# One PSUM tile for each bank of the down products, and TensorE in source order, in a two-layer encoder step

## The chip, the cores and the metric

One core of a Trainium2 chip runs the whole program. The metric is the device time of one execution in microseconds (us); lower is better. Engines are named as in the profile: PE is TensorE (PEld its weight loads), DVE is VectorE, ACT is ScalarE, POOL is GpSimd, SP is SyncE.

## The reference

An inference step of a two-layer encoder with D_MODEL = 1024 and D_FF = 4096, for 512 tokens of a new stream and 64 of a running one. Layer 0 mixes tokens by a causal pooling mixer, layer 1 by sparse attention with an indexer; after each mixer comes a squared-ReLU MLP, each with an RMSNorm ahead and a residual add behind:

```
def _mlp(h, w_up, w_down):
    u = jax.nn.relu(h @ w_up)
    return (u * u) @ w_down
...
        x = x + y.astype(x.dtype)
        x = x + _mlp(_rmsnorm(x, norm_mlp[i]), mlp_w_up[i], mlp_w_down[i]).astype(x.dtype)
```

All arrays are float32. The change concerns the two MLPs.

## The kernel before

**Data.** The residual x lies feature-major in SBUF: eight tiles x[k] of 128 features by 576 tokens, handled in two halves of 288 tokens. To keep float32 accuracy each float32 operand is split in two parts, a rounded one and a remainder, and each product is three matmuls (high by high, high by low, low by high) for each 128 x 128 block of weights and each half of the tokens. The parts of a weight are wh (a copy on ACT, L166) and wl (a subtraction on DVE, L167; in the first two up tiles of MLP 0 on POOL). xs are the two parts of the normalised input before its scale by the row statistics.

**Stages.** The kernel runs pool_mixer, mlp(0), attention and mlp(1) one after the other; `stage` opens the SBUF pools of each. PSUM has eight banks: pool ps holds three tiles of two banks, po two tiles of one bank, for the whole kernel.

**An MLP.** `mlp` (L320) works in four chunks of D_FF. A chunk has eight up tiles: `project` (L226, matmuls on L234) takes 48 matmuls into a two-bank tile `up`. `activated` reads it on DVE (v, L327: ReLU and the scale 1/rms of each token) and squares on ACT (L328); `factors` (L335) makes, of two up tiles, the seven sums that Strassen's scheme needs (L341-348). The scale of the tokens, norm.rb, is ready late: Norm.add sums the squares of x over its eight tiles into s2 (L252; on POOL for the first ones of MLP 0, on DVE otherwise), `stats` takes column sums with ten small matmuls (L284) and 1/sqrt by ACT (rt, L301) and DVE (L303-308), `spread` puts them on all partitions (diagonals on DVE, L274; matmuls rb, L264; copy on ACT, L265). No v can be computed before that, so the first up tiles stay in PSUM until then. In the source, `stats` stands behind the first up tile, `spread` behind the second.

**The down of a chunk.** Where chunk c is below `strassen` (all four in MLP 0, three in MLP 1), down(c) multiplies by Strassen's scheme: four objects `Pair` (L359), each with seven products of 12 matmuls into three banks a, b and c. The opening makes b11 on a, t2 on b, t1 on c; then DVE reads each bank (L380 or L382 for a, L383 for b, L384 for c). The closing accumulates four more: b21 on a, t3 on b, b22 on c, t4 on b, and after each of them DVE adds the bank to the residual (L396). So b takes two products in the closing, with a read between. a and b are the two banks of one ps tile `ab`, c is a po tile. The last chunk of MLP 1 is a plain product, its final norm is in `last` (L452).

**Weights.** `made` (L170) yields units in the order of use: a block of up weights is one load of 512 KB (raw, L125) and two units; a pair of down weights is two loads (pair, L183), and POOL makes sums of their quarters (L186, L187, L191, L194) for seven units a11, s2, s1, a12, a21', s2', a22. The loads are issued from ACT's queue. Units rotate through a ring of eight buffers, so wh of a unit waits until TensorE has used the unit eight before. The raws have two buffers, and one pair is in work at a time.

**Order.** The source is a program in order; a scheduler (Tile's) then orders each engine's instructions by its own simulated time and priorities, and puts in the semaphore waits. Each engine executes its own instructions in that order. Only `with tc.manual_schedule(engines=...)` keeps the source order for the engines named, as in `last` for PE. In the MLPs before the change the scheduler orders PE: it starts the next pair's opening before the pair before has closed, begins the next up tile in the tail of a down, and starts attention's first projections in the last down of MLP 0. The statistics of MLP 0 land in the third up tile, behind 35 of its 48 matmuls, those of MLP 1 in the second, behind ten.

Of the kernel before, what the change touches and what calls it, by code (L numbers as in the profile page):

```python
# [9 lines left out]
F32 = mybir.dt.float32  # L10
# [3 lines left out]
ENG = mybir.EngineType  # L14
PSUM = bass.MemoryType.PSUM

P = 128
D = 1024
KT = D // P
# [24 lines left out]
def pool_dsa_kernel(ctx: ExitStack, tc: tile.TileContext, a, o):  # L44
    nc = tc.nc
    act, dve, pool, pe = nc.scalar, nc.vector, nc.gpsimd, nc.tensor
# [4 lines left out]
    raws = ctx.enter_context(tc.tile_pool(name="raws", bufs=2))  # L51
    norms = ctx.enter_context(tc.tile_pool(name="norms", bufs=1))
    tiny = ctx.enter_context(tc.tile_pool(name="tiny", bufs=4))
    ps = ctx.enter_context(tc.tile_pool(name="ps", bufs=3, space=PSUM))
    po = ctx.enter_context(tc.tile_pool(name="po", bufs=2, space=PSUM))
    dram = ctx.enter_context(tc.tile_pool(name="dram", bufs=1, space=bass.MemoryType.DRAM))

    count = [0]
# [1 line left out]
    def uid(s):  # L60
        count[0] += 1
        return f"{s}_{count[0]}"

    phase = {}

    @contextmanager
    def stage(**pools):

        with ExitStack() as st:
            phase.clear()  # L70
            for name, bufs in pools.items():
                phase[name] = st.enter_context(tc.tile_pool(name=uid(name), bufs=bufs, reuse_waits="tile"))
            yield

    def slot(tag, s, dt=F32R):
# [13 lines left out]
        return tiny.tile([P, n], F32, tag=s, name=uid(s))  # L89

    def psum(s="ps"):
        return ps.tile([P, 2, 512], F32, tag="ps", name=uid(s))

    def psum1(s="po"):
        return po.tile([P, 512], F32, tag="po", name=uid(s))

    def f32(t):
        return t.bitcast(F32)
# [1 line left out]
    def halves(t):  # L100
        return t.rearrange("p (h t) -> p h t", h=2)
# [108 lines left out]
    def next_block(sub=dve):  # L210
        return [next_unit(5 - i, sub) for i in range(2)]

    def at(w, k):

        return [t[:, (k % 4) * P:(k % 4 + 1) * P] for t in w[k // 4]]
# [10 lines left out]
    def project(pt, w, xs, between=iter(()), cols=((0, HT), (HT, HT))):  # L226

        n = len(xs)
        for k in range(n):
            next(between, None)  # L230
            wh, wl = at(w, k)
            for i, (wt, part) in enumerate(((wh, 0), (wh, 1), (wl, 0))):
                for h, (c, m) in enumerate(cols):
                    pe.matmul(  # L234
                        pt[:, h, :m], wt, xs[k][:, part, c:c + m],
                        start=(k == 0 and i == 0), stop=(k == n - 1 and i == 2),
                    )

    class Norm:
# [14 lines left out]
        def stats(self):  # L254
            pt = psum1("st")
            token_sums(pt, self.s2)
            self.r = rms(pt)

        def spread(self):
            diag = diagonals(self.r)  # L260
            self.rb = tmp("rb" + self.s, "rb", 1)
            for h in range(2):
                pb = psum1("rb")
                pe.matmul(pb[:, :HT], ones, diag[:, h * HT:(h + 1) * HT], start=True, stop=True)  # L264
                act.copy(self.rb[:, h * HT:(h + 1) * HT], pb[:, :HT])  # L265
            return self.rb
# [44 lines left out]
    def split_x(gi, norm, tags, add=dve):  # L311
        xs = []
        for k in range(KT):
            t = pair_slot(tags[k], "xs")
            split(t, x[k], gv[:, gi, k:k + 1])
            norm.add(k, add if k < 6 else dve)
            xs.append(t)
        return xs

    def mlp(layer, gi, strassen, add=dve, end=None):  # L320
        norm = Norm(f"m{layer}")
        xs = split_x(gi, norm, ["xs"] * KT, add)
# [7 lines left out]
        def plain(pt, u):  # L330
            v = halves(tmp("v"))
            activated(pt, v)
            split(u.rearrange("p a (h t) -> p a h t", h=2), v)
# [25 lines left out]
        class Pair:  # L359


            def __init__(self, c, q, us):
                self.c, self.q, self.us = c, q, us
                ab = psum("ab")
                self.a, self.b, self.c_ = ab[:, 0], ab[:, 1], psum1("c")
                self.lo, self.hi = ([x[2 * q + i][:, c0:c0 + HT] for i in range(2)] for c0 in (HT, 0))

            def opening(self, parts=((0, 1, 2, 3),)):
# [29 lines left out]
        def down(c, us):  # L398
            for q in range(KT // 2):
                p = Pair(c, q, us)  # L400
                for _ in p.opening(((0, 1, 2, 3),) if q else ((0, 1, 2), (3,))):
                    pass
                p.closing()
# [3 lines left out]
        def finished(c, i, pt, us):  # L407
            nonlocal v
            f = UP_ORDER[i]
            if c < strassen:  # L410
                if i % 2 == 0:
                    v = phase["acts"].tile([P, 4, HT], F32, tag="v", bufs=1, name=uid("v"))
                activated(pt, v[:, 2 * (i % 2):2 * (i % 2) + 2])
                if i % 2:
                    us[i // 2] = factors(v)
            else:
                if i % 3 == 0:
                    v = phase["u"].tile([P, 7 * 2 * HT], F32R, tag="u", bufs=4, name=uid("u"))
                us[f] = v[:, (i % 3) * SLOT:(i % 3 + 1) * SLOT].rearrange("p (h t) -> p h t", h=2)
                plain(pt, us[f])  # L420

        us = [[None] * KT for _ in range(4)]
        todo = []
        steps = [s for c in range(4) for s in [(c, i) for i in range(c > 0, 8)] + ([(c + 1, 0)] if c < 3 else []) + [(c, None)]]
        for n, (c, i) in enumerate(steps):
            if i is not None:
                w = next_block(sub=add if n < 2 else dve)
                pt = psum("up")
                project(pt, w, xs)
                todo.append((c, i, pt, us[c]))  # L430
                if n == 0:
                    norm.stats()
                    continue
                if n == 1:
                    norm.spread()
                for t in todo:
                    finished(*t)
                todo.clear()
                continue
            if c < strassen:  # L440
                down(c, us[c])
                continue
            for m in range(KT if end is None or c < 3 else KT - LAST):
                w = next_block()
                pt = psum("dn")
                project(pt, w, us[c])
                dve.tensor_tensor(halves(x[m]), halves(x[m]), pt[:, :, :HT], ALU.add)
# [675 lines left out]
            dve.tensor_tensor(x[m][:, 2 * P:], x[m][:, 2 * P:], pt[:, 0, :T - 2 * P], ALU.add)  # L1123

    x = Residual()
    with stage(slots=1, xs=1, tmps=6):
        pool_mixer()
    with stage(u=1, xs=1, acts=1, tmps=3, pairs=1, more=2):
        mlp(0, 1, 4, pool)
    with stage(slots=1, xs=1, cst2=1, tmps=6):  # L1130
        attention()
    with stage(xs=1, u=1, acts=1, tmps=3, pairs=1, more=2):
        mlp(1, 3, 3, end=last)


# [94 lines left out]
```

## Time and profile before

| | us |
|---|---|
| median of 3 runs (lowest to highest) | 1165.96 (1164.63 to 1166.82) |
| profiled execution | 1169.65 |
| its span, first to last instruction | 1167.8 |
| mean granted clock of TensorE | 0.980 |
| busy: PE / DVE / ACT / POOL | 1110.5 / 817.0 / 528.9 / 349.9 |

The span is 1.85 us shorter than the execution's own time. Rows of a timeline give start, duration, engine, line, operation, output and inputs; "x3" groups three instructions; a bracket gives the idle time of the engine before it and what ended it. In the view of one line, "its engine sat idle before it" lists total us and times by releaser. In tables of stretches come the busy times of each engine, the granted clock (1.00 is full speed), the DMA share and GB/s. L-numbers are lines of the kernel before; tile names stand without their numbers.

### The profile page before, as it was taken

The page shows a single profiled execution, that of the slowest core. Times are in us where ns is not written, and L with a number is a line of the kernel's source. Part 1 is how long each engine was busy: PE and PEld are TensorE (multiplying, and loading weights), DVE is VectorE, ACT ScalarE, POOL GpSimd, SP SyncE. Part 2 cuts the span into 40 slices and gives each one's busy share as a digit, 9 for nine tenths or more (in the row PEclk, how much of TensorE's full clock was granted, in tenths as well). Part 3 has the DMA queues.
Part 4 walks back from the last instruction along what each step waited for, and adds up shares of the span by engine and source line. Part 5 has one row for each costly group of instructions (what it writes and reads, how often), then busy time and mean ns, then how long its engine had stood idle before and what let it go on. Part 6 is the DMA issues. An engine that isn't in the chain of part 4 may idle for free.

```text
span 1167.8 us, 20621 instructions
## 1 busy us (share of the span) xinstructions
PE 1110.5 (95%) x8244; PEld 1090.6 (93%) x8244; DVE 817.0 (70%) x1478; ACT 528.9 (45%) x968; POOL 349.9 (30%) x274
## 2 busy tenths in 40 slices
PE   7999999999999999798989999999999999989995
PEld 6999999999999999797979999999999989989995
DVE  7776666767667786759999853876766767775434
ACT  5644344335334444253368665654344335333331
POOL 7711410330240351117775341101410330350002
PEclk8999999999999999798989999999999999999998
DMA  5421241232232134366652432431241132114212
GB/s 172 114 75 52 73 145 55 75 125 73 73 108 91 38 113 161 101 197 158 170 154 74 121 104 81 157 109 55 73 145 55 57 125 90 55 55 122 77 37 82
DMA packets 51152, 116.68 MB, mean 100 GB/s; under 512 B 9345, under 2 KB 22960, under 8 KB 51056
## 3 DMA queue, kind: packets, MB, share of 16 engines
q10 hardware_dynamic: 23184, 84.45, 23.1%
q1 hardware_dynamic: 27872, 30.90, 9.2%
q8 instruction: 65, 1.06, 0.4%
q14 instruction: 31, 0.25, 0.1%
HBM read 99.73 MB, written 13.25 MB: 97 GB/s over the span
## 4 chain that ended last, share of the span: by engine, by line
PE 60%; DVE 15%; issue 12%; POOL 5%; DMA 4%; ACT 3%; SPq 0%; DVEq 0%; ACTq 0%; POOLq 0%
PE up L234 30%; PE ab L356 8%; DVE wl L167 5%; PE dn L234 4%; PE pj L234 4%; PE c L356 3%; DVE work L896 2%; PE o L971 2%; DMA raw<-in_w_up 2%; PE wa L234 1%; DMA pair<-in_w_down 1%; DVE m L895 1%; POOL sum L194 1%; PE v L1088 1%; PE pb L720 1%
## 5 line engine op out<-in xcount | busy, mean ns | idle before, releaser
L234 PE MATMUL up<-xs,wh 128*128 128x288 f32 x2048 | 355.9, 295 | 1.5 <-DVE v L327 1.3
L234 PEld LDWEIGHTS up<-xs,wh 128*128 128x128 f32 x2048 | 299.8, 188 | 2.5 <-DVE v L327 1.7
L356 PE MATMUL ab<-u,wh 128*128 128x288 f32 x1120 | 227.2, 297 | 11.4 <-DVE x L396 5.8
L166 ACT CAST wh<-raw 128x512 fp32r<-128x512 f32 (+1 forms) x210 | 126.0, 619 | 206.2 <-DMA raw<-in_w_up 61.9
L234 PE MATMUL up<-xs,wl 128*128 128x288 f32 x1024 | 219.4, 295 | 0.0
L167 DVE TENSOR_TENSOR wl<-raw,wh 128x512 fp32r<-128x512 f32 (+1 forms) x186 | 144.3, 784 | 70.7 <-ACT wh L166 68.9
L356 PEld LDWEIGHTS ab<-u,wh 128*128 128x128 f32 x1120 | 179.4, 189 | 15.3 <-DVE x L396 8.6
L356 PE MATMUL ab<-u,wl 128*128 128x288 f32 x560 | 165.5, 298 | 2.0 <-DVE wl L167 1.9
L234 PEld LDWEIGHTS up<-xs,wl 128*128 128x128 f32 x1024 | 164.2, 188 | 0.0
L167 DVE TENSOR_TENSOR wl<-pair,wh 128x512 fp32r<-128x512 f32 x112 | 101.4, 917 | 30.5 <-ACT wh L166 30.0
L194 POOL TENSOR_TENSOR sum<-sum,pair 128x512 f32<-128x512 f32 x28 | 41.2, 1472 | 265.4 <-DVE wl L167 265.4
L186 POOL TENSOR_TENSOR sum<-pair 128x512 f32<-128x512 f32 x28 | 38.0, 1357 | 266.7 <-DMA pair<-in_w_down 266.7
L166 ACT CAST wh<-sum 128x512 fp32r<-128x512 f32 x84 | 51.0, 621 | 145.8 <-POOL sum L187 47.7
L356 PEld LDWEIGHTS ab<-u,wl 128*128 128x128 f32 x560 | 105.4, 189 | 3.9 <-DVE wl L167 3.5
L166 ACT CAST wh<-pair 128x512 fp32r<-128x512 f32 x112 | 68.2, 620 | 86.4 <-PE up L234 40.7
L356 PE MATMUL c<-u,wh 128*128 128x288 f32 x448 | 92.5, 295 | 0.4 <-ACT wh L166 0.4
L167 DVE TENSOR_TENSOR wl<-sum,wh 128x512 fp32r<-128x512 f32 x84 | 71.2, 858 | 26.2 <-ACT wh L166 25.4
L327 DVE SCALAR_TENSOR_TENSOR v<-up,rbm 128x576 f32<-128x576 f32 x64 | 48.2, 755 | 58.6 <-PE up L234 57.2
L234 PE MATMUL pj<-xs,wh 128*128 128x288 f32 x448 | 83.5, 304 | 4.1 <-DVE t L783 4.1
L234 PEld LDWEIGHTS pj<-xs,wh 128*128 128x128 f32 x448 | 70.1, 197 | 5.8 <-DVE t L783 4.9
L356 PEld LDWEIGHTS c<-u,wh 128*128 128x128 f32 x448 | 72.4, 189 | 0.7 <-ACT wh L166 0.7
L356 PE MATMUL c<-u,wl 128*128 128x288 f32 x224 | 66.0, 296 | 0.0
(224 smaller groups left out, 1974.6 us busy)
## 6 DMA issues: line engine op xcount, KB each, us to landing
raw<-in_w_up ACTq DMA_DIRECT2D x64, 512.0 KB, 3.6
pair<-in_w_down ACTq DMA_DIRECT2D x56, 512.0 KB, 3.6
raw<-in_w_o ACTq DMA_DIRECT2D x16, 512.0 KB, 4.1
raw<-in_w_in ACTq DMA_DIRECT2D x15, 512.0 KB, 4.0
q<-st SPq DMA_DIRECT2D x32, 144.0 KB, 2.6
q<-q SPq DMA_DIRECT2D x16, 256.0 KB, 3.0
raw<-in_w_down ACTq DMA_DIRECT2D x8, 512.0 KB, 3.5
x<-in_x SPq DMA_DIRECT2D x8, 288.0 KB, 6.3
```

Of the source, the lines that this page charges most:

```text
L166: act.copy(h, src)
L167: how["sub"].tensor_tensor(l, src, f32(h), ALU.subtract)
L186: pool.tensor_tensor(s1, a21, a22, ALU.add)
L194: pool.tensor_tensor(s2, s2, a12, ALU.add)
L234: pe.matmul(pt[:, h, :m], wt, xs[k][:, part, c:c + m], start=(k == 0 and i == 0), stop=(k == n - 1 and i == 2),)
L327: dve.scalar_tensor_tensor(v, pt[:, :, :HT], 0.0, halves(norm.rb), ALU.max, ALU.mult)
L356: pe.matmul(bank[:, :HT], wt, ut, start=first and j == 0 and i == 0, stop=last and j == 3 and i == 2, skip_group_check=True)
L720: pe.matmul(pt[:, c0:c0 + rhs.shape[1]], lhs, rhs, start=n == 0, stop=n == len(steps) - 1)
L895: dve.max(m8[:np_], wk[:np_])
L896: dve.match_replace(wk[:np_], m8[:np_], wk[:np_], TAKEN)
L971: pe.matmul(oc[:, 2 * s + hh], pT[:, c:c + P], V[:, kt, vs], start=kt == 0, stop=kt == i)
L1088: pe.matmul(pt[:n, :264], xs[k][:, part, i * P:i * P + n], wt[:, sl], start=(k == 0 and j == 0), stop=(k == KT - 1 and j == 2))
```

## The change

The pools ps and po are opened for each stage. pool_mixer and attention get ps = 3 and po = 2, as before; both MLPs get ps = 2 (two tiles of two banks) and po = 4 (four tiles of one bank): eight banks in each case. A Pair's a, b and c become three tiles of one bank. Both calls of mlp stand in manual_schedule for PE, so TensorE executes an MLP in the order of the source: a pair's seven products (the first pair's opening in two parts) before the next pair's, a down before the next up tile, and attention behind the last down. `norm.stats()` moves from behind the first up tile to the middle of the second, behind 30 of its 48 matmuls. No instruction is added or removed on any engine's work; on POOL and SP the order is nearly unchanged, on DVE and ACT it changes locally.

```diff
@@ pools and stages @@
-    ps = ctx.enter_context(tc.tile_pool(name="ps", bufs=3, space=PSUM))
-    po = ctx.enter_context(tc.tile_pool(name="po", bufs=2, space=PSUM))
...
             for name, bufs in pools.items():
-                phase[name] = st.enter_context(tc.tile_pool(name=uid(name), bufs=bufs, reuse_waits="tile"))
+                space = {"space": PSUM} if name in ("ps", "po") else {}
+                phase[name] = st.enter_context(tc.tile_pool(name=uid(name), bufs=bufs, reuse_waits="tile", **space))
...
-        return ps.tile([P, 2, 512], F32, tag="ps", name=uid(s))
+        return phase["ps"].tile([P, 2, 512], F32, tag="ps", name=uid(s))
...
-        return po.tile([P, 512], F32, tag="po", name=uid(s))
+        return phase["po"].tile([P, 512], F32, tag="po", name=uid(s))
@@ class Pair @@
-                ab = psum("ab")
-                self.a, self.b, self.c_ = ab[:, 0], ab[:, 1], psum1("c")
+                self.a, self.b, self.c_ = (psum1(t) for t in "abc")
@@ mlp @@
+        def sums():
+
+            for k in range(KT):
+                if k == KT // 2 + 1:
+                    norm.stats()
+                yield
+
...
-                project(pt, w, xs)
+                project(pt, w, xs, sums() if n == 1 else iter(()))
                 todo.append((c, i, pt, us[c]))
                 if n == 0:
-                    norm.stats()
                     continue
@@ calls @@
-    with stage(slots=1, xs=1, tmps=6):
+    with stage(slots=1, xs=1, tmps=6, ps=3, po=2):
         pool_mixer()
-    with stage(u=1, xs=1, acts=1, tmps=3, pairs=1, more=2):
-        mlp(0, 1, 4, pool)
-    with stage(slots=1, xs=1, cst2=1, tmps=6):
+    with stage(u=1, xs=1, acts=1, tmps=3, pairs=1, more=2, ps=2, po=4):
+        with tc.manual_schedule(engines={ENG.PE}):
+            mlp(0, 1, 4, pool)
+    with stage(slots=1, xs=1, cst2=1, tmps=6, ps=3, po=2):
         attention()
-    with stage(xs=1, u=1, acts=1, tmps=3, pairs=1, more=2):
-        mlp(1, 3, 3, end=last)
+    with stage(xs=1, u=1, acts=1, tmps=3, pairs=1, more=2, ps=2, po=4):
+        with tc.manual_schedule(engines={ENG.PE}):
+            mlp(1, 3, 3, end=last)
```

## The prediction

> **What bounds the kernel now.** I read the page first: the busy time of the engines.
>
> ```profile
> PE 1110.5 (95%) x8244; PEld 1090.6 (93%) x8244; DVE 817.0 (70%) x1478; ACT 528.9 (45%) x968; POOL 349.9 (30%) x274
> ```
>
> TensorE works for 95% of the span. The change keeps every matmul, so the time can move only through TensorE's idle time. What Strassen's down products wait for is in the view of line L356.
>
> ```profile
>   DVE x L396: 5.8, 11
>   ACT wh L166: 3.3, 3
>   DVE u L347: 2.1, 1
>   DVE wl L167: 1.9, 5
>   DVE x L383: 0.7, 1
> ```
>
> That is 13.8 us (the second number is how often) in seven downs. 6.5 of it (L396 and L383) are waits for VectorE to read a bank, 5.2 waits for weights, 2.1 a wait for factors. The end of a matmul in the trace is modelled, some 0.16 us after the next one's start, so each of the 20 waits besides L347's is worth 0.16 more: 8.4 us for banks, 6.5 for weights, 14.9 together. This is the most that the downs can give. L347's wait (the last factors before the down of chunk 3) depends neither on banks nor on the order, and stays.
>
> The unit of all that follows is the matmul step. A product is 12 of them:
>
> ```profile
> 225.32 0.42 PE L356 MATMUL c<-u,wh 128*128 128x288 f32 x2
> ...
> 226.90 0.42 PE L356 MATMUL ab<-u,wh 128*128 128x288 f32 x2
> ```
>
> 1.58 us, 0.132 a matmul, and 6.35 for an up tile of 48.
>
> **Part 1: the statistics of MLP 0.** Before, they are in the third up tile, after 35 of its 48 matmuls.
>
> ```profile
> 65.84 1.16 PE L284 MATMUL st<-ones,s 128*128 128x2 f32 x10
> ...
> 69.17 1.24 PE L264 MATMUL rb<-diag,ones 128*128 128x288 f32 x4 [0.25 <-DVE diag L274]
> 71.69 0.53 PE L234 MATMUL up<-xs,wh 128*128 128x288 f32 x2 [1.29 <-DVE v L327]
> ```
>
> Counted back from 65.84, the third tile began at 61.2, the second at 54.85. The change puts the statistics after 30 matmuls of the second: TensorE comes to them at 58.8. Their input s2 ends on a chain over POOL and VectorE:
>
> ```profile
> 59.89 1.88 POOL L252 TENSOR_TENSOR s<-s,sq 128x576 f32<-128x576 f32 x1
> ```
>
> ```profile
> 61.80 0.76 DVE L252 TENSOR_TENSOR s<-s,sq 128x576 f32<-128x576 f32 x1 [1.32 <-POOL s L252]
> 62.48 0.68 DVE L167 TENSOR_TENSOR wl<-raw,wh 128x512 fp32r<-128x512 f32 x1
> 63.08 0.75 DVE L252 TENSOR_TENSOR s<-s,sq 128x576 f32<-128x576 f32 x1
> ```
>
> The change keeps POOL's order here; on VectorE the wl (0.60 from start to start) no longer stands between the two adds. So s2 is there at about 63.3 rather than 63.83, and TensorE waits about 4.5 us, in order, with 18 ready matmuls of the second tile and the whole third tile behind the wait. From the statistics on the chain stays: they began at 65.84, and the next up tile 5.85 later, when a v had been written out of its PSUM buffer. It is now the third tile, not the fourth, that waits for this, because the MLPs have two buffers of two banks where there were three. With the statistics at 63.5 it starts at 69.4. Two tiles are then done; before, three were at 71.69. At 69.4 + 6.35 = 75.75 TensorE is as far as it was at 71.69: **4.1 us lost**.
>
> The clock can add to it. L347's wait of 2.1 us, and the stretches behind it (length, busy time of PE, PEld, DVE, ACT, POOL, then the granted clock):
>
> ```profile
> 401.65 0.61 PE L356 MATMUL ab<-u,wh 128*128 128x288 f32 x1 [2.06 <-DVE u L347]
> ```
>
> ```profile
> 402.00:403.00 1.00, 1.00 (x5) 1.00 (x5) 1.00 (x1) 0.62 (x1) 0.00 (x0) 0.50 0.00 0
> 403.00:404.00 1.00, 1.00 (x6) 1.00 (x6) 1.00 (x3) 0.62 (x1) 0.12 (x1) 0.50 0.03 8
> 404.00:405.00 1.00, 1.00 (x6) 1.00 (x6) 0.98 (x3) 0.79 (x2) 1.00 (x1) 0.50 0.00 0
> ```
>
> Three us at half the clock, 1.5 us of work. The new gap of 4.5 us is longer than the one before these rows, so I expect the same; as a part of the slow stretch falls into the time in which TensorE waits for rb anyway, I take 1.2, between 0 and 1.5.
>
> **Part 2: the statistics of MLP 1.**
>
> ```profile
> 757.46 0.75 DVE L252 TENSOR_TENSOR s<-s,sq 128x576 f32<-128x576 f32 x1
> ...
> 767.48 1.42 DVE L327 SCALAR_TENSOR_TENSOR v<-up,rbm 128x576 f32<-128x576 f32 x2 [0.46 <-ACT rbm L265]
> ```
>
> ```profile
> 760.53 0.33 ACTq L125 DMA_DIRECT2D raw<-in_w_up  x1
> 762.16 1.14 ACT L166 CAST wh<-raw 128x512 fp32r<-128x512 f32 x2 [2.47 <-DMA raw<-in_w_up]
> 763.21 0.40 ACT L301 ACTIVATE rt<-st,eps 128x4 f32<-128x4 f32 x2
> ```
>
> ```profile
> 758.68 1.15 PE L284 MATMUL st<-ones,s 128*128 128x2 f32 x10
> ...
> 766.64 0.90 PE L234 MATMUL up<-xs,wh 128*128 128x288 f32 x4
> ```
>
> s2 is there at 758.2; ten matmuls of the second tile stand before the statistics at 758.68, so 30 put them at 761.3 without a wait on TensorE. But ScalarE has a chain of weight loads ahead of rt. In the changed order one more wh stands there, the one whose raw is issued at 760.53 and lands some 3.6 later (row below), 764.1: rt goes from 763.2 to about 765.2, and with it diag, rb and the first v, which ended at 767.48 + 0.71 = 768.2, to about 770.1. Before, the third buffer let the third up tile start without that v, at 767.0 (within the row at 766.64); now it waits for it: **3.1 us lost**, between 1.2 (rt not delayed) and 4. Half of a slow stretch on top, 0.7, between 0 and 1.5.
>
> **Part 3: the downs.** Groups and loads that their price needs (busy, mean ns of one):
>
> ```profile
> L167 DVE TENSOR_TENSOR wl<-pair,wh 128x512 fp32r<-128x512 f32 x112 | 101.4, 917 | 30.5 <-ACT wh L166 30.0
> L194 POOL TENSOR_TENSOR sum<-sum,pair 128x512 f32<-128x512 f32 x28 | 41.2, 1472 | 265.4 <-DVE wl L167 265.4
> L186 POOL TENSOR_TENSOR sum<-pair 128x512 f32<-128x512 f32 x28 | 38.0, 1357 | 266.7 <-DMA pair<-in_w_down 266.7
> ...
> raw<-in_w_up ACTq DMA_DIRECT2D x64, 512.0 KB, 3.6
> pair<-in_w_down ACTq DMA_DIRECT2D x56, 512.0 KB, 3.6
> ```
>
> In source order a pair's last four products are b21 on bank a, t3 on b, b22 on c, t4 on b again. t4 may not start before VectorE has added t3's bank to the residual, and only b22 lies between: from t3's end VectorE has 1.58 us. The read itself is 0.45, but VectorE takes its instructions in order, and remainders of weights (L167) and the read of bank a stand before it. Such a pile did this before:
>
> ```profile
> 227.00 1.71 DVE L167 TENSOR_TENSOR wl<-sum,wh 128x512 fp32r<-128x512 f32 x2 [1.03 <-ACT wh L166]
> 228.64 1.78 DVE L167 TENSOR_TENSOR wl<-pair,wh 128x512 fp32r<-128x512 f32 x1
> 230.34 0.44 DVE L396 TENSOR_TENSOR x<-x,c 128x288 f32<-128x288 f32 x1
> 230.70 0.44 DVE L396 TENSOR_TENSOR x<-x,ab 128x288 f32<-128x288 f32 x1
> ```
>
> The product on c that ended by 227.0, and the one on ab after it, were read at 230.34 and 230.70, two to three us late. TensorE lost nothing there, because the order before had the next pair's opening (up to three products, 4.75 us) to do meanwhile. The changed order has none of it between t3 and t4: that cover is what it gives up. Per pair, from the start of its b11: second weight load issued after 0.4, landed after 4.0, two POOL sums of 1.3 (the mean of 1.36 has the slow ones of the start in it), wh 0.6 (1.14 for two, above), then in VectorE's new order wl 0.92, a's read 0.45, two wl of 0.85 (from the pile's 1.71), t3's read 0.45: 10.7. t4 is due after six products, 9.5, so it waits 1.2 us. The same walk with each pair's own order on VectorE gives 0.35 for pair 0, 1.2 (MLP 0) to 2.1 for pair 1, 0.95 to 2.2 for pair 2, and nothing for pair 3, where no sums stand in between. For the seven downs: 2.5 three times and 4.2 in MLP 0, 3.8, 3.8 and 4.65 in MLP 1: 24.0 us, where 14.9 go. **9.1 us lost.** An error of 0.5 us at each of the 21 waits moves this by 10.5 either way, and nothing excludes a gain up to the whole 14.9.
>
> The separate tiles of a, b and c let a bank go when its own read ends; that is within the 8.4 us. That attention's first projections (57 of their matmuls lay in the last down) now follow it takes none of their work away, and attention's entry waits for VectorE either way: I count nothing.
>
> **The sum.** 4.1 + 1.2 + 3.1 + 0.7 + 9.1 = 18.2. The profiled execution took 1169.65 (its span 1167.8 and 1.85 around it), so it would be 1187.85; it was 3.7 above the median of the runs, 1165.96, to which I add the same 18.2: **1184 us**.
>
> **Rivals.**
> - *The banks pay* (faster). If t3's read always ends within 1.58 us, because the sums come early enough that only reads stand before it, TensorE loses no time at t4; and products in the order in which weights are made release the ring in order, so the 6.5 us of weights go too. For it: the waits for L396 are the largest item, and VectorE is idle for 30% of the span. Against it: the pile at 227. Starts +7.2 (without the clock) to +9.1, downs −10 to −15: 1158 to 1165, taken as 1161. It decides at a wait of 0.28 us at each of the 21: at 5.8 us of new waits the downs' gain of 9.1 equals the starts' loss.
> - *The downs come out even*: new waits of 0.7 us at each of the 21. Only the starts count: 1166 + 9 = 1175.
> - *The clock follows the waits.* Five of the 21 new waits come out at 2 us or more (pair 1 in MLP 1, pair 2 in the last chunks), as long as L347's 2.1. If each of them is followed by three us at half the clock, as that one was, 5 x 1.5 = 7.5 us more: 18.2 + 7.5 = 25.7, 1192. For it: the rows at 402. Against it: one such wait in the downs before is all there is to go by, and my five are walked to 0.5 us. [...]
> - *The starts cost nothing*, if s2 were there at 59 rather than 63.3, and the downs are even: no change. POOL's add from 59.89 and the two after it speak against it.
>
> **Chances.** Forecast 0.42, its own range 1179 to 1190; even downs 0.20; clock 0.16; banks pay 0.17; starts free 0.05. A measurement of this kernel tells about 0.2%, 2.3 us, from no change. Faster 0.17, same 0.05, slower 0.78. The range reaches from the upper half of the faster case to the clock's case and a few us over it, for waits longer than walked: 1162 to 1198.
>
> **What would show it.** In the changed profile: L284 waits 4 to 5 us for DVE L252 at 59, and the third up tile starts at about 69.4 after a v (part 1); in MLP 1 rt stands at 765 and the third up tile at 770, after a v (part 2); L356 waits for x some 18 to 22 times, 0.3 to 2.2 us each, on b, and hardly for wh or wl (part 3). I am wrong if t3's reads end before b22 does, or if the waits for weights grow instead, because the sums' remainders come late in VectorE's new order.

## The result, and the profile after

The changed kernel takes 1206.64 us in the median of four runs (1202.82 to 1210.6), against 1166.39 for the kernel before (1164.63 to 1171.1): a ratio of 1.0339, 95% interval 1.0294 to 1.0384. It is about 40 us slower; 18 were forecast. The direction was right, the size was not. The profiled execution of the changed kernel took 1210.6 us, with a span of 1208.8, 41.0 more than before.

The page of the changed kernel, its head and the row of slices for the clock (tenths of full speed in 40 slices):

```profile
span 1208.8 us, 20641 instructions
...
PE 1121.2 (93%) x8244; PEld 1101.9 (91%) x8244; DVE 824.5 (68%) x1478; ACT 532.6 (44%) x968; POOL 355.6 (29%) x274
...
PEclk8989999999999998899889999999999999999998
```

The same row of the kernel before:

```profile
PEclk8999999999999999798989999999999999999998
```

PE executes the same 8244 matmuls and is busy 10.7 us longer, so some of them ran slower; there are more 8s in the clock's row, and the mean granted clock is 0.969 (0.980 before). The rest of the 41 us is idle time. What TensorE waits for (total, times, longest):

```profile
PE b L356 <- DVE x L395: 34.4, 23, 6.1
...
PE up L234 <- DVE x L1128: 3.6, 1, 3.6
PE up L234 <- DVE v L327: 3.3, 2, 1.9
PE a L356 <- DVE u L347: 3.3, 1, 3.3
PE st L284 <- DVE s L252: 3.1, 1, 3.1
```

(L395 is L396 of the kernel before, L1128 its L1123.) The forecast wait at t4 is there, on b, 23 times; no product waits for wh or wl any more. Only it is 34.4 us and not 24.0. The stages, taken from the matmuls in the timelines, show where the 41 us are; the last two columns belong to experiments below.

| stretch, us | before | changed | changed, sums on DVE | before, sums on DVE |
|---|---|---|---|---|
| pool mixer's last matmul to first down | 61.3 | 68.4 | 64.2 | 60.4 |
| first down to attention's statistics | 358.1 | 378.1 | 356.6 | 348.8 |
| these to attention's last matmul | 283.0 | 281.5 | 280.2 | 283.1 |
| attention's last matmul to MLP 1's first down | 60.3 | 66.5 | 62.6 | 59.1 |
| first down to the plain product | 290.0 | 298.9 | 289.7 | 279.5 |
| plain product to the last matmul | 58.2 | 58.5 | 58.6 | 58.6 |

The two starts lose 7.1 and 6.2 us, the downs 20.0 and 8.9. The start of MLP 0, on PE:

```profile
49.68 0.76 PE L234 MATMUL up<-xs,wh 128*128 128x288 f32 x4 [1.13 <-DVE x L733]
63.40 2.18 PE L284 MATMUL st<-ones,s 128*128 128x2 f32 x10 [3.14 <-DVE s L252]
72.41 0.77 PE L234 MATMUL up<-xs,wh 128*128 128x288 f32 x4 [1.37 <-DVE v L327]
```

The statistics stand at 63.40, where 63.5 was forecast. But the ten matmuls take 2.18 us where they took 1.16, and the third up tile comes at 72.41, not at 69.4. Stretches of the granted clock (third number from the right) say why, here and in four of the downs:

```profile
64.00:65.00 1.00, 1.00 (x6) 1.00 (x6) 0.00 (x0) 0.00 (x0) 0.00 (x0) 0.50 0.00 0
66.00:67.00 1.00, 1.00 (x6) 1.00 (x5) 0.82 (x6) 0.02 (x1) 0.00 (x0) 0.50 0.00 0
68.00:69.00 1.00, 1.00 (x6) 1.00 (x5) 0.00 (x0) 0.00 (x0) 0.00 (x0) 0.50 0.00 0
343.00:344.00 1.00, 1.00 (x6) 1.00 (x5) 0.94 (x2) 0.00 (x0) 0.00 (x0) 0.50 0.81 328
462.00:463.00 1.00, 1.00 (x6) 1.00 (x6) 1.00 (x2) 0.17 (x1) 0.00 (x0) 0.50 0.00 0
968.00:969.00 1.00, 1.00 (x6) 1.00 (x5) 0.22 (x1) 0.00 (x0) 0.00 (x0) 0.50 0.60 242
1071.00:1072.00 1.00, 1.00 (x6) 1.00 (x6) 0.42 (x2) 0.00 (x0) 0.00 (x0) 0.50 0.59 217
```

Six matmuls in a us, at half the clock, where a busy us of the up tiles at 1.00 has nine or ten. Busy time times the missing clock, summed over stretches of 1 us, is 15.1 us in the two MLPs (3.2 and 1.5 at the starts, 10.5 in the downs) against 1.6 before, all of it in one down.

One pair of the second chunk shows what t4 waits for. VectorE:

```profile
235.35 1.41 DVE L167 TENSOR_TENSOR wl<-pair,wh 128x512 fp32r<-128x512 f32 x1
236.90 1.56 DVE L167 TENSOR_TENSOR wl<-sum,wh 128x512 fp32r<-128x512 f32 x1
238.39 0.44 DVE L395 TENSOR_TENSOR x<-x,a 128x288 f32<-128x288 f32 x1
238.76 1.62 DVE L167 TENSOR_TENSOR wl<-sum,wh 128x512 fp32r<-128x512 f32 x1
240.30 0.68 DVE L167 TENSOR_TENSOR wl<-pair,wh 128x512 fp32r<-128x512 f32 x1
240.90 0.44 DVE L395 TENSOR_TENSOR x<-x,b 128x288 f32<-128x288 f32 x1
```

POOL and PE at the same time:

```profile
234.92 1.29 POOL L187 TENSOR_TENSOR sum<-sum,pair 128x512 f32<-128x512 f32 x1
236.18 1.75 POOL L191 TENSOR_TENSOR pair<-pair,pair 128x512 f32<-128x512 f32 x1
238.55 1.28 POOL L194 TENSOR_TENSOR sum<-sum,pair 128x512 f32<-128x512 f32 x1 [0.62 <-DVE wl L167]
```

```profile
239.26 0.29 PE L356 MATMUL c<-u,wl 128*128 128x288 f32 x1
241.49 0.50 PE L356 MATMUL b<-u,wh 128*128 128x288 f32 x2 [1.93 <-DVE x L395]
```

b22 is done at 239.55, t3's read ends at 241.34, t4 starts at 241.49. Ahead of the read stand four remainders. The one at 240.30, with POOL idle, takes 0.68. The three that overlap an addition of POOL take 1.41, 1.56 and 1.62, and each of them ends about 0.55 us after that addition: 236.76 after 236.21, 238.46 after 237.93, 240.38 after 239.83. They look like instructions that stand still until POOL is done. The read of a bank takes 0.44 us beside POOL and without it. The experiments ask whether this is the cause.

The longest wait of the 23, 6.08 us up to 461.05, has another beginning. The second load of its pair was issued at 444.81, and POOL's first sum could start only at 452.19, 7.4 us later (the median from issue to landing is 3.6); VectorE then sat idle for weights, and the remainders came after that.

```profile
452.19 1.29 POOL L186 TENSOR_TENSOR sum<-pair 128x512 f32<-128x512 f32 x1 [3.78 <-DMA pair<-in_w_down]
```

```profile
454.17 0.69 DVE L167 TENSOR_TENSOR wl<-sum,wh 128x512 fp32r<-128x512 f32 x1 [3.47 <-ACT wh L166]
```

Why this load took so long was not tried.

### The profile page after: what moved, and what is told of

Same layout as the page of the kernel before. It is cut to its first block, busy times and chain, and to the rows that moved or that the text cites. A ratio compares the mean times of both kernels' runs of the same rounds, so it can differ in the third digit from the quotient of the medians.

```text
span 1208.8 us, 20641 instructions
## 1 busy us (share of the span) xinstructions
PE 1121.2 (93%) x8244; PEld 1101.9 (91%) x8244; DVE 824.5 (68%) x1478; ACT 532.6 (44%) x968; POOL 355.6 (29%) x274
## 4 chain that ended last, share of the span: by engine, by line
PE 62%; issue 15%; DVE 12%; POOL 6%; ACT 3%; DMA 1%; ACTq 0%; SPq 0%; DVEq 0%; POOLq 0%
PE up L234 30%; PE b L356 5%; PE pj L234 5%; DVE wl L167 4%; PE dn L234 4%; PE a L356 3%; PE o L976 2%; PE wa L234 2%; PE c L356 2%; ACT wh L166 2%; POOL sum L187 1%; POOL sum L186 1%; DVE work L901 1%; POOL sum L194 1%; PE v L1093 1%
## 5 line engine op out<-in xcount | busy, mean ns | idle before, releaser
L167 DVE TENSOR_TENSOR wl<-raw,wh 128x512 fp32r<-128x512 f32 (+1 forms) x186 | 147.8, 798 | 79.5 <-ACT wh L166 74.2
L356 PE MATMUL b<-u,wh 128*128 128x288 f32 x672 | 142.9, 305 | 35.2 <-DVE x L395 34.4
L356 PEld LDWEIGHTS b<-u,wh 128*128 128x128 f32 x672 | 110.5, 194 | 40.9 <-DVE x L395 22.7
L186 POOL TENSOR_TENSOR sum<-pair 128x512 f32<-128x512 f32 x28 | 38.9, 1389 | 263.1 <-DMA pair<-in_w_down 237.4
L356 PE MATMUL b<-u,wl 128*128 128x288 f32 x336 | 101.4, 302 | 0.0
L356 PE MATMUL a<-u,wh 128*128 128x288 f32 x448 | 94.8, 304 | 3.3 <-DVE u L347 3.3
L356 PE MATMUL c<-u,wh 128*128 128x288 f32 x448 | 91.1, 295 | 0.0
L356 PEld LDWEIGHTS a<-u,wh 128*128 128x128 f32 x448 | 75.4, 197 | 3.5 <-DVE u L347 3.5
L356 PEld LDWEIGHTS c<-u,wh 128*128 128x128 f32 x448 | 72.0, 189 | 0.0
```

What stands on the lines that cost most here:

```text
L167: how["sub"].tensor_tensor(l, src, f32(h), ALU.subtract)
L186: pool.tensor_tensor(s1, a21, a22, ALU.add)
L356: pe.matmul(bank[:, :HT], wt, ut, start=first and j == 0 and i == 0, stop=last and j == 3 and i == 2, skip_group_check=True)
```

## The experiments

**Theories.** A: TensorE's source order takes away the cover between t3 and t4, and that is the loss. B (rival): the PSUM layout costs (two two-bank buffers, pools opened for each stage). C (rival to A, formed from the rows above): the loss comes from the weights' sums, by POOL's work beside VectorE or by lateness; the source order only uncovers it. Times are medians in the order of the runs; a ratio is to the kernel before, on the same chip.

**1 to 3. The parts alone.** 1, the layout without the order:

```diff
-                project(pt, w, xs, sums() if n == 1 else iter(()))
+                project(pt, w, xs)
...
                 if n == 0:
+                    norm.stats()
                     continue
...
-        with tc.manual_schedule(engines={ENG.PE}):
-            mlp(0, 1, 4, pool)
+        mlp(0, 1, 4, pool)
...
```

> The changed kernel with the scheduler ordering TensorE again and the statistics back in their old place: only the PSUM layout is left of the change. If the source order is what costs (theory), the waits for x L395 fall from 34.4 us to under 8 and the time is 1160 to 1172, the starts paying up to 4 us for the missing third two-bank buffer. If the layout costs (rival: two two-bank buffers, pools opened for each stage), it stays above 1185.

2, the order and the moved statistics without the layout:

```diff
...
-                project(pt, w, xs)
+                project(pt, w, xs, sums() if n == 1 else iter(()))
...
-        mlp(0, 1, 4, pool)
+        with tc.manual_schedule(engines={ENG.PE}):
+            mlp(0, 1, 4, pool)
...
```

> The kernel before with TensorE in source order in both MLPs and the statistics amid the second up tile, but with its own PSUM layout for the whole kernel. Theory: the waits at t4 are there as in the changed kernel (30 us or more for x) and the time is 1190 to 1205; less than the changed kernel only by its new waits at the entries of the MLPs (1.1 and 3.6 us). Rival (layout): under 1175.

3, only the pools opened for each stage, at their old sizes:

```diff
...
-    with stage(u=1, xs=1, acts=1, tmps=3, pairs=1, more=2):
+    with stage(u=1, xs=1, acts=1, tmps=3, pairs=1, more=2, ps=3, po=2):
...
```

> The kernel before with its PSUM pools opened for each stage, at the old sizes. If a pool that opens waits for the last reader of the pools before it, the first up tile of MLP 1 stands about 3.6 us later and that of MLP 0 about 1.1: 1167 to 1171. If the two entry waits come from the source order alone, no change, 1166.

Measured: 1187.43 us for the layout alone (1.0165, 1.0138 to 1.0191), 1250.91 for the order alone (1.0699, 1.0678 to 1.0721), 1172.21 for the pools alone (1.0040, 1.0025 to 1.0055). The first comes out where theory B has it, the second far beyond what theory A has, the third a us above its range. The order alone costs 84 us, twice the whole change. Its waits:

```profile
PE ab L356 <- DVE x L396: 48.8, 29, 4.0
PE ab L356 <- DVE x L383: 9.5, 8, 3.3
PE st L284 <- DVE s L252: 6.3, 2, 4.4
```

Where a and b are one tile, a read of one bank held up the product on the other (one t3, on b, starts at 247.12, released by the read of a that began at 246.53), and in source order nothing covers it; against this kernel the changed one is 44 us faster. So the two parts of the change are not additive. The layout alone loses 6.5 and 5.5 us in the starts, and 12.9 from MLP 0's first down to attention's statistics, where TensorE still waits for x L395 (9.0 us on b, 8 times, in both MLPs) and on c (2.6); in MLP 1's downs it gains 2.6. The pools for each stage cost 4.9: the first up tile of MLP 1 waits 3.5 us for the last read of attention's last tile, and that of MLP 0 for 1.1.

**4, 7, 12. The starts.** 4, the statistics behind all of the second up tile:

```diff
-                project(pt, w, xs, sums() if n == 1 else iter(()))
+                project(pt, w, xs)
...
                 if n == 1:
+                    norm.stats()
                     norm.spread()
```

> The changed kernel with the statistics behind all 48 matmuls of the second up tile. Theory: in MLP 0 the wait for s2 falls from 3.1 to about 0.8 us and the slow clock behind it goes, 2 to 4 us gained there; in MLP 1, where the statistics did not wait, the third up tile starts about 2 us later: 1203 to 1207 in all. Rival (the slow clock there does not hang on the wait): the clock is 0.5 from 63 on again and the time 1207 to 1211.

7, matmuls that nobody needs, in the wait for s2:

```diff
+                    if layer == 0:
+                        fill = psum1("fill")
+                        for j in range(24):
+                            pe.matmul(fill[:, :HT], xs[0][:, 0, :P], xs[0][:, 0, :HT], start=j == 0, stop=j == 23)
+                        act.copy(small(1, "fill"), fill[:, :1])
                     norm.stats()
```

> The changed kernel with 24 idle matmuls (128x288, into a one-bank tile of their own, 3.2 us) ahead of the statistics of MLP 0, where TensorE waits 3.1 us for s2 and the clock is then halved for six us. If the halved clock hangs on that wait, it stays at 1.00 there, the first down starts 2 to 3 us earlier than 68.4 us after the pool mixer's last matmul, and the time is 1203 to 1205. If it does not, the first down starts as before and the time is 1206 to 1208.

12, the order of the pools:

```diff
-    with stage(u=1, xs=1, acts=1, tmps=3, pairs=1, more=2, ps=2, po=4):
+    with stage(u=1, xs=1, acts=1, tmps=3, pairs=1, more=2, po=4, ps=2):
...
```

> The changed kernel with po opened ahead of ps in both MLPs, so that the first up tile lies on other banks than the last tiles of the stage before. If its wait at the entries (1.1 us in MLP 0, 3.6 us in MLP 1, with a slow clock behind it) is for the one tile that held those banks, it goes or shrinks: 1201 to 1205. If a new pool waits for everything before it, no change: 1206 to 1208.

Measured: 1209.31 (1.0348, 1.0326 to 1.0369), 1202.39 (1.0295, 1.0277 to 1.0313) and 1208.63 (1.0351, 1.0313 to 1.0388). The changed kernel's own interval overlaps all three. Late statistics no longer wait for s2, but then rb waits for diag and the clock is halved from 65 to 75 all the same; MLP 1's start grows from 66.5 to 72.6. With the filling matmuls the clock stays at 1.00 until the first v is waited for (1.89 us), and is halved then; the stretches of that kernel:

```profile
62.00:65.00 3.00, 3.00 (x24) 2.73 (x23) 1.14 (x6) 0.56 (x3) 0.00 (x0) 1.00 0.09 34
65.00:68.00 3.00, 2.51 (x16) 1.94 (x14) 1.85 (x5) 1.02 (x2) 0.00 (x0) 1.00 0.00 0
70.00:72.00 2.00, 2.00 (x10) 2.00 (x9) 1.79 (x5) 1.65 (x3) 0.00 (x0) 0.50 0.30 123
```

So the halved clock at 63 did follow from the idle time, as that expectation has it, but the first down comes only 0.7 us earlier (67.7 for 68.4): the slow stretch moved to the next wait. With po first the waits for L733 and L1128 are gone, and the starts are 68.7 and 66.0 us, much the same. In MLP 0 TensorE then waits 4.5 us for s2 instead. In MLP 1 rt now stands behind a wh that waits for its load:

```profile
794.58 0.62 ACT L166 CAST wh<-raw 128x512 fp32r<-128x512 f32 x1 [1.45 <-DMA raw<-in_w_up]
795.11 0.40 ACT L301 ACTIVATE rt<-st,eps 128x4 f32<-128x4 f32 x2
```

That is 3.2 us behind the start of the statistics (791.95), 1.2 in the changed kernel, and the clock falls behind the wait for v (0.57 from 800 to 804). What sets the starts is the chain to the first v, which the third up tile needs when there are only two buffers: in MLP 0 from s2 on, in MLP 1 by way of rt. To take away a wait ahead of it gains 0.7 us at most in these three runs.

**5, 6, 9, 11. The cover, and VectorE's order.** 5, the next pair's b11 between b22 and t4:

```diff
+            def first(self):
+                self.started = True
+                product(self.a, next_unit(), self.us, "b11", (0, 1, 2, 3), True, True)
...
-                    product(bank, next_unit(), self.us, factor, js, False, True)
+                    w = next_unit()
+                    if factor == "t4" and following:
+                        following.first()
+                    product(bank, w, self.us, factor, js, False, True)
```

> The changed kernel with the next pair's b11 (12 matmuls into the fourth one-bank tile, free then) put between b22 and t4, so that VectorE has 3.2 us and not 1.6 for t3's read. Theory (t4 lacks cover): of the 34.4 us of waits for x L395 only what is longer than 1.6 stays, some 10 us, and the slow clock behind the short ones goes: 1175 to 1185. Rival (VectorE and the weights are late as such): the waits move to the opening or to wh and wl, and the time stays above 1195.

6, t3 first in the closing:

```diff
+            yield split_unit(a21)
             yield split_unit(a12)
-            yield split_unit(a21)
...
-                for bank, factor, out, b2 in ((self.a, "b21", self.lo[0], 0), (self.b, "t3", self.hi[1], 0),
+                for bank, factor, out, b2 in ((self.b, "t3", self.hi[1], 0), (self.a, "b21", self.lo[0], 0),
```

> The changed kernel with t3 ahead of b21 in the closing (and the unit a21' made ahead of a12), so that two products lie between t3 and t4, but only one between t2 and t3 on the same bank. Theory: the waits at t4 go as with the cover, but t3 now waits for POOL's sum a21' and for the read of t2: 1180 to 1195. Rival: no gain, 1200 or more.

9, VectorE in source order in the downs of the changed kernel (11: of the kernel before, with VectorE alone):

```diff
+                with tc.manual_schedule(engines={ENG.PE, ENG.DVE}):
                     for _ in p.opening(((0, 1, 2, 3),) if q else ((0, 1, 2), (3,))):
                         pass
                     p.closing()
```

> The changed kernel with VectorE, too, in source order inside the downs: t3's read then stands behind one remainder after b21's read, not behind two or three. TensorE's order is the changed kernel's. If VectorE's order makes t3's read late, the waits for x fall to 10 to 15 us, some come back as waits for wl, and the time is 1180 to 1195. If the missing cover alone decides, it stays at 1200 to 1210.

> The kernel before with VectorE alone in source order inside the downs, TensorE left to the scheduler: reads of banks stand ahead of more of the remainders. If VectorE's order costs the kernel before its 8 us of bank waits too, 1158 to 1164; if the remainders then come late for TensorE instead, 1166 to 1180.

Measured: 1197.36 (1.0247, 1.0222 to 1.0271), 1191.66 (1.0198, 1.0174 to 1.0222), 1204.34 (1.0322, 1.0269 to 1.0374) and 1192.83 (1.0212, 1.0196 to 1.0227). The waits of 5:

```profile
PE b L356 <- DVE x L404: 26.8, 17, 5.2
```

(L404 is the same addition.) Twice the cover takes 7.6 of the 34.4 us away, where theory A expected 24. t3 first, with two products between t3 and t4, comes out in theory A's range: it leaves 11.0 for the closing's reads and makes 11.5 for the opening's. VectorE in source order has 23.2 for x and 5.6 for wh, and no clear gain. In the kernel before, the scheduler's order of VectorE was the better one by 24 us, more than either range of 11 had. So cover is worth something, and 6 is the best of the kernels in source order that keep the sums on POOL; but theory A in its plain form, that one product more between t3 and t4 mends it, fell here: VectorE is later than that.

**8, 10, 15. The sums taken away.** These three leave out the use of POOL's four sums of each pair: the units are made from the plain quarters, so the results are not those of the step, and only the times count. 8 and 15 have no additions (changed kernel and kernel before), 10 is the changed kernel with the additions made into tiles that nothing reads. The edit of 8 and 15:

```diff
...
-            pool.tensor_tensor(s1, a21, a22, ALU.add)
-            pool.tensor_tensor(s2, s1, a11, ALU.add)
             yield split_unit(a11)
-            yield split_unit(s2)
-            yield split_unit(s1)
-            pool.tensor_tensor(a21, a21, a11, ALU.add)
+            yield split_unit(a21)
+            yield split_unit(a21)
             yield split_unit(a12)
             yield split_unit(a21)
-            pool.tensor_tensor(s2, s2, a12, ALU.add)
-            yield split_unit(s2)
+            yield split_unit(a12)
```

> The changed kernel without POOL's sums of weights: the four additions of a pair are left out and their units are made from the plain quarters, so VectorE and ScalarE do as many splits, but nothing waits for POOL and nothing of POOL runs beside VectorE. If the waits at t4 come from the remainders that VectorE must do ahead of t3's read, late by POOL's sums and slowed beside them (the pile's wl of 1.4 to 1.8 us where I reckoned 0.85), they fall below 10 us and the time to 1170 to 1180. If the strict order of TensorE is enough by itself, more than 20 us of waits stay and the time is above 1190.

> As the run without POOL's sums (units from the plain quarters), but POOL still makes its four additions a pair into tiles that nothing reads: nothing waits for them, they only run beside VectorE. If it is the work beside VectorE that makes the pile (wl of 1.4 to 1.8 us), waits come back and the time is 1165 to 1185; if it is that the sums come late, it stays at 1153 to 1158.

> The kernel before without POOL's sums of weights (left out; units from the plain quarters), beside the changed kernel without them, 1153. If the source order costs nothing by itself once the pile is gone, this gives 1140 to 1150, that is better than 1153 by the starts alone (some 5 to 10 us); if the source order is still worth something against it, over 1155.

Measured: 1153.36 (0.9864, 0.9849 to 0.9879), 1219.83 (1.0438, 1.0419 to 1.0457) and 1140.30 (0.9750, 0.9730 to 0.9770). 8 gains more than expected, 10 loses more. What the downs wait for in 8 (the view of the products' line, with its other numbers):

```profile
  DVE x L378: 2.7, 2
  DVE x L390: 1.2, 4
  DVE u L343: 1.0, 1
```

and what TensorE waits for in 10:

```profile
PE b L356 <- DVE x L395: 30.3, 24, 3.3
PE c L356 <- DVE x L383: 15.0, 13, 1.7
```

Both have TensorE in source order, the same splits and loads, and no product that needs a sum. In 8 the waits for x are 3.9 us, in 10 they are 45.3. What differs is that POOL works beside VectorE. VectorE's order does not: by their names, 1473 of its 1478 instructions stand in the same order in both. The remainders show it; the group of 8, then that of 10:

```profile
L167 DVE TENSOR_TENSOR wl<-pair,wh 128x512 fp32r<-128x512 f32 x196 | 136.9, 707 | 64.3 <-ACT wh L166 63.8
```

```profile
L167 DVE TENSOR_TENSOR wl<-pair,wh 128x512 fp32r<-128x512 f32 x196 | 190.6, 981 | 72.0 <-ACT wh L166 72.0
```

707 ns each against 981. So it is POOL's work beside VectorE, not that the sums come late. Between 15 and 8 lie 13 us: without the pile the change still costs 2.2 and 3.1 us in the starts, 5.9 from MLP 0's first down to attention, and 1.3 or less in each other stretch. The change by itself is nearly free in MLP 1's downs (280.9 for 279.9 us).

**13, 14. The sums on VectorE.** All work is kept; 13 is the kernel before, 14 the changed one.

```diff
-            pool.tensor_tensor(s1, a21, a22, ALU.add)
-            pool.tensor_tensor(s2, s1, a11, ALU.add)
+            dve.tensor_tensor(s1, a21, a22, ALU.add)
+            dve.tensor_tensor(s2, s1, a11, ALU.add)
...
-            pool.tensor_tensor(a21, a21, a11, ALU.add)
+            dve.tensor_tensor(a21, a21, a11, ALU.add)
...
-            pool.tensor_tensor(s2, s2, a12, ALU.add)
+            dve.tensor_tensor(s2, s2, a12, ALU.add)
```

> The kernel before with the four additions of each pair of weights on VectorE and not on POOL; all work is kept. 112 additions of about 0.7 us are 78 us more for VectorE, while its 196 remainders of the downs lose what they pay beside POOL (0.89 in the mean against 0.69 alone: 39 us). If POOL's work beside VectorE is what delays reads and weights, 1155 to 1165; if VectorE becomes the bound in the downs, 1170 to 1190.

> The changed kernel with the same additions on VectorE; all work is kept. If the waits at t4 hang on POOL's work beside VectorE, they fall below 15 us and the time to 1170 to 1185, though VectorE has 78 us more to do; if they hang on the amount of VectorE's work ahead of t3's read, they stay above 30 us and the time at 1200 to 1230.

Measured: 1146.94 for 13 (0.9811, 0.9796 to 0.9827), better than expected, and 1170.93 for 14 (1.0026, 1.0009 to 1.0044). 13 beats both kernels by 1.9% and more. Its groups on VectorE:

```profile
L167 DVE TENSOR_TENSOR wl<-pair,wh 128x512 fp32r<-128x512 f32 x112 | 78.1, 704 | 23.8 <-ACT wh L166 23.2
L167 DVE TENSOR_TENSOR wl<-sum,wh 128x512 fp32r<-128x512 f32 x84 | 58.5, 703 | 4.9 <-ACT wh L166 4.2
L186 DVE TENSOR_TENSOR sum<-pair 128x512 f32<-128x512 f32 x28 | 21.3, 759 | 11.7 <-DMA pair<-in_w_down 11.0
```

An addition of L186 takes 0.76 us here and took 1.36 on POOL, the remainders fall from 917 and 858 to 704 and 703 ns, and the products wait 1.3 us in all, where they waited 13.8. The wait at t4 in 14:

```profile
PE b L356 <- DVE x L395: 13.5, 15, 2.4
```

It was 34.4 us, 23 times: VectorE does 112 instructions more, many of them ahead of the same reads, and is still in time more often. Between 13 and 14 the change costs 24.0 us, where it costs 40 with the sums on POOL and 13 without any. So some 16 of the 40 us hang on POOL making the sums, and theory C is half right: the order and the layout cost by themselves too.

## Why the prediction was wrong, point by point

- **Which engine, which wait: right.** t4 waits for t3's read, on b, 23 times (18 to 22 expected), hardly any wait for wh or wl is left, and remainders stand ahead of the read.
- **The price of a remainder: wrong, and the main step that failed.** The walk of part 3 has "wl 0.92 ... two wl of 0.85 (from the pile's 1.71)". These are means over two kinds, and the line view of the changed kernel shows them: most at 0.69 us, and those beside POOL.

```profile
L167 DVE TENSOR_TENSOR wl<-pair,wh x112: 676/691/1784, 95.3 to 1085.0; 128x512 fp32r<-128x512 f32 x112
L167 DVE TENSOR_TENSOR wl<-sum,wh x84: 677/683/1621, 98.8 to 1085.6; 128x512 fp32r<-128x512 f32 x84
```

  (Least, median and most, ns.) Of these 196 remainders 141 take 0.7 us or less. All 53 that take over 0.9 overlap an instruction of POOL, and 49 of the 53 stand between the start of b21 and t3's read. In the pair shown above the walk's three, from 236.90 on, took 1.56, 1.62 and 0.68 us, 3.9 where I had 2.6, and t4 waited 1.93 us where I had 1.2. The row of 1.78 stood in the prediction, and I reckoned with the mean. The waits for x alone came to 34.4 us, where I had 24.0 for all waits of the downs; 6.1 of it is the wait with the late load, which I did not have at all. Runs 8, 10 and 14 show the cause: without additions beside VectorE the waits for x are 3.9 us, with additions that nothing needs 45.3, and with the additions on VectorE itself 13.5 at t4.
- **The clock: a rival that came true in part.** "The clock follows the waits" had 0.16. In the downs five slow stretches cost 10.5 us (1.6 before). This is 8.9 of the 28.9 us that the downs and attention's entry lost, beside some 24.7 more of waits (38.5 at L356 for 13.8), with 4.7 us given back elsewhere, among them the 2.3 us that attention's statistics waited before.
- **The start of MLP 0: the place right, the size not.** 4.1 + 1.2 were forecast, 7.1 measured: the statistics came at the forecast time, but the slow clock cost 3.2 and not 1.2, and it lengthened the chain to the third tile, which I had kept at 5.85 us (9.0 measured): rb comes behind the 18 matmuls that were left of the second tile, and could start only at 69.90.
- **The start of MLP 1: 6.2 for 3.8, by another way.** rt did not wait for a late wh: it followed the statistics at once. The first up tile waited 3.6 us for attention's last read; with po opened first, so that the tile lies on other banks, that wait is gone (run 12). I had not seen it; run 3 shows its price where three buffers hide the rest, 4.9 us in all, and run 12 that it is not the last bound in the changed kernel. There, without that wait, the one that I had described comes: rt behind a late wh, 2.0 us later.
- **"The banks pay": no, but they help.** With TensorE in source order the new layout saves 44 us (run 2 against the changed kernel). With the scheduler's order the layout gained 2.6 us in MLP 1's downs, while MLP 0's took 12.9 us longer up to attention's statistics (run 1).
- **Attention's entry: "I count nothing" holds for the kernel as it is** only roughly: without sums the change loses 5.9 us from MLP 0's first down to attention's statistics. How much of that is the order of the projections was not tried alone.

## What to carry to other kernels

An engine's mean for one instruction can hide two kinds (here remainders of 0.69 us and of up to 1.78); ahead of a wait that decides, take the duration of those instances that stand there, beside the work that runs with them. Work moved to an idle engine is not free when it slows the busy one: here 112 additions cost less on VectorE, which was then 71 to 73% busy, than on POOL (0.9811 and 1.0026 of the kernel before's time, for 1 and 1.0339). And before a scheduler's order is replaced by the source's, look for what each product on a shared bank has between itself and the one before; here the strict order paid 34.4 us for late reads of b, and the slow stretches behind the waits of the downs cost 10.5 us again.

## What the runs showed of the hardware

- A remainder on VectorE, with both inputs in SBUF, took 0.68 to 0.70 us where POOL did nothing and up to 1.78 beside an addition on POOL (the changed kernel). Each of the 53 that took over 0.9 us ended 0.55 us after an instruction of POOL, among them the one of 1.62 us at 238.76. An addition of a PSUM bank to x (L395) took 0.44 to 0.46 us in all 112 cases, 29 of them beside POOL. What in the chip makes the difference was not tried.
- The clock was halved behind five of six waits of 2.4 us or more in the downs of the changed kernel (2.44, 3.26, 6.08, 2.60 and 3.22 us; not behind one of 2.80), and behind none of those up to 1.93. In run 14 no down shows it, with a longest wait of 2.4. A wait's length alone does not decide it: in run 14 the first up tile of MLP 0 starts behind a wait of 1.12 us at half the clock (0.50 from 49 to 51), in the changed kernel behind one of 1.13 at the full one (1.00 from 50 on). The seven slow stretches at the starts and in the downs of the changed kernel lasted 3.4 us (from 342.8, 779.8, 967.5 and 1069.9) or 6.8 us (from 63.0, 421.4 and 458.9), worked out from the clock of each us around them.
